# Mean-square pooling on one core: joined square roots, and one sum over groups of four for six of the twenty loads

## The chip, the core and the metric

The kernel runs on one core of a Trainium2 chip. Time is device time in microseconds (us) of one execution; of several executions the median is given. The profiled execution is a further one, and its trace covers a span that is somewhat shorter than its time.

## The reference

The input x has the shape (32, 256, 4096) in float32, p is 2.0 and the kernel size is 4. Each output is a power mean over four neighbours:

```python
for i in range(out_length):
    start = i * kernel_size
    end = start + kernel_size
    window = np.abs(x[:, :, start:end]) ** p
    result[:, :, i] = (np.mean(window, axis=-1)) ** (1.0 / p)
```

So out = sqrt((a*a + b*b + c*c + d*d) / 4): 134.22 MB are read from HBM and 33.55 MB are written, with four squares, three adds and one root for each output.

## The kernel before

**Tiles.** The flat input is cut into 20 loads: 19 of 128 partitions x 13184 values (6592 KB) and a last one of 11648. Three buffers of that size, xt0 to xt2 (`X_SLOTS = 3`), take them in turn, so load i+3 goes into the buffer of load i and can be issued only when load i has been summed. Output blocks 0 to 3 hold four loads each; their results stand side by side in one tile ot (4 x 3296 values a partition, `place`, line 69). One store of 6592 KB sends a block out. Loads 16, 17 and 18 form a fifth block and load 19 a sixth; their results go into the buffer of load 17, which no later load needs.

**Steps of a load.** ScalarE squares it in place (`square`, line 88). VectorE adds in two instructions: `pairs` (line 94) adds values 0 and 1 of each four to values 2 and 3, 13184 to 6592 in place; `fours` (line 98) adds the two that are left, 6592 to 3296. ScalarE takes the root with the scale 1/4 (`root`, line 101) into ot. Since ot is still being stored when the first load of the next block is ready, the sums of loads 4, 8, 12 and 16 go to a PSUM tile st (`summed`, line 103), and only the root moves them to ot, which then has to wait for the store. The sums of loads 5, 9 and 13 are the first to be written into ot by VectorE, and wait for the same store.

**Order.** The order is written by hand (`tc.manual_schedule()`); each engine works through its own list. In the loop over loads 0 to 16 (line 114), ScalarE does square(i) and then the root of load i-1; for i = 4, 8 and 12 the root of i-1 goes ahead of square(i), so that the store of the finished block can be issued. Stores 0 to 2 are issued by ScalarE's queue, right after the root that fills the block (line 108). SyncE's queue issues the loads, and after load 19 the stores 3, 4 and 5. An instruction in a queue waits behind those in front of it.

**Tail.** After the loop, load 17 is squared and summed, and loads 18 and 19 are squared by both engines: VectorE multiplies the first 4608 or 2000 values by themselves (line 134), ScalarE squares the others. Then come the last sums, roots and stores.

**Dependencies.** The waits follow from the tiles that instructions write and read. `tc.declare_no_dep` takes out one of them where others already ensure it; the kernel before uses it in `shared_pairs` alone.

Of the kernel before, what the change touches and what calls it, by code (L numbers as in the profile page):

```python
# [1 line left out]

# [4 lines left out]


@with_exitstack
def kernel(  # L10
    ctx: ExitStack,
    tc: tile.TileContext,
    x: bass.AP,
    p: float,
    kernel_size: int,
    out: bass.AP,
):

    nc = tc.nc

    assert float(p) == 2.0, "kernel specialized for p == 2"
    k = int(kernel_size)  # L30
    assert k == 4, "kernel specialized for kernel_size == 4"

    P = nc.NUM_PARTITIONS
    fp32 = mybir.dt.float32
    Act = mybir.ActivationFunctionType
    add = mybir.AluOpType.add
    xf = x.rearrange("b c l -> (b c l)")
    of = out.rearrange("b c l -> (b c l)")
    total = xf.shape[0] // P

    W = 13184
    R = W // k
    X_SLOTS = 3
    LAST = total - 19 * W
    widths = [W] * 19 + [LAST]
    n = len(widths)
    assert 0 < LAST <= W and LAST % 16 == 0


    blocks = [[0, 1, 2, 3], [4, 5, 6, 7], [8, 9, 10, 11], [12, 13, 14, 15], [18, 16, 17], [19]]  # L50
    block_of = {i: b for b, group in enumerate(blocks) for i in group}
    block_width = [sum(widths[i] for i in group) for group in blocks]

    x_pool = ctx.enter_context(tc.tile_pool(name="x_pool", bufs=1))
    o_pool = ctx.enter_context(tc.tile_pool(name="o_pool", bufs=1))
    s_pool = ctx.enter_context(tc.tile_pool(name="s_pool", bufs=1, space=bass.MemoryType.PSUM))
    x_tiles = [x_pool.tile([P, W], fp32, name=f"xt{j}") for j in range(X_SLOTS)]
    o_tile = o_pool.tile([P, 4 * R], fp32, name="ot")
    first = o_pool.tile([P, 1], fp32, name="first")
    s_tile = s_pool.tile([P, 4096], fp32, name="st")  # L60
    ctx.enter_context(tc.manual_schedule())

    def rows(flat, b, div):
        at = sum(block_width[:b]) * P // div
        return flat[at:at + block_width[b] * P // div].rearrange("(p w) -> p w", p=P)


    free = x_tiles[17 % X_SLOTS]
    place = {i: o_tile[:, i % 4 * R:(i % 4 + 1) * R] for i in range(16)}
    place[18] = free[:, R:2 * R]  # L70
    place[19] = free[:, 0:LAST // k]
    place[16] = free[:, 2 * R:3 * R]
    place[17] = free[:, 3 * R:4 * R]
    held = [o_tile[:, :]] * 4 + [free[:, R:4 * R], place[19]]

    xs, loads = {}, {}

    def load(i):
        b = block_of[i]
        at = sum(widths[j] for j in blocks[b][:blocks[b].index(i)])  # L80
        xs[i] = x_tiles[i % X_SLOTS][:, 0:widths[i]]
        loads[i] = nc.sync.dma_start(out=xs[i], in_=rows(xf, b, 1)[:, at:at + widths[i]])  # L82

    def store(b, queue):
        queue.dma_start(out=rows(of, b, k), in_=held[b])  # L85

    def square(v):
        return nc.scalar.activation(out=v, in_=v, func=Act.Square)  # L88

    def pairs(v):  # L90

        q = v.rearrange("p (n j) -> p n j", j=k)
        h = v[:, 0:v.shape[1] // 2].rearrange("p (n j) -> p n j", j=2)
        return nc.vector.tensor_tensor(out=h, in0=q[:, :, 0:2], in1=q[:, :, 2:4], op=add)  # L94

    def fours(o, v):
        h = v[:, 0:v.shape[1] // 2].rearrange("p (n j) -> p n j", j=2)
        return nc.vector.tensor_tensor(out=o, in0=h[:, :, 0], in1=h[:, :, 1], op=add)  # L98

    def root(o, s):  # L100
        nc.scalar.activation(out=o, in_=s, func=Act.Sqrt, scale=1.0 / k)  # L101

    summed = {i: s_tile[:, 0:R] if i in (4, 8, 12, 16) else place[i] for i in range(n)}

    def roots(i):
        root(place[i], summed[i])
        if i in (3, 7, 11):
            store(block_of[i], nc.scalar)

    for i in range(X_SLOTS):  # L110
        load(i)

    root(first[:, :], nc.const_aps.tensor(1.0, (P, 1), fp32))
    for i in range(17):
        ends = i in (4, 8, 12)
        if ends:
            roots(i - 1)
        square(xs[i])
        if i and not ends:
            roots(i - 1)  # L120
        pairs(xs[i])
        fours(summed[i], xs[i])
        if i + X_SLOTS < n:
            load(i + X_SLOTS)

    store(3, nc.sync)
    square(xs[17])
    pairs(xs[17])
    fours(summed[17], xs[17])
    later = {18: 4608, 19: 2000}  # L130

    def shared_square(i):
        v = xs[i][:, 0:later[i]]
        nc.vector.tensor_tensor(out=v, in0=v, in1=v, op=mybir.AluOpType.mult)  # L134
        square(xs[i][:, later[i]:widths[i]])

    def shared_pairs(i):
        tc.declare_no_dep(pairs(xs[i]).ins, loads[i].ins, reason="the two squares waited for it")

    shared_square(18)  # L140
    roots(16)
    roots(17)
    shared_pairs(18)
    fours(summed[18], xs[18])
    shared_square(19)
    roots(18)
    store(4, nc.sync)
    shared_pairs(19)
    fours(summed[19], xs[19])
    roots(19)  # L150
    store(5, nc.sync)


# [1 line left out]
_INS = ['x', 'p', 'kernel_size']  # L155
_OUTS = [((32, 256, 1024), 'float32')]

_NUMBERS = {'p': 2.0, 'kernel_size': 4}


# [26 lines left out]
```

## Time and profile before

| what | value |
|---|---|
| three executions | 394.27, 394.32, 394.55 us; median 394.32 us |
| profiled execution | 394.39 us |
| its span in the trace | 392.4 us |
| moved by DMA | 134.22 MB read and 33.55 MB written |
| ScalarE: 20 squares, 20 roots | 216.7 us and 58.6 us |
| VectorE: 20 `pairs`, 20 `fours`, 2 multiplications | 139.7, 71.5 and 7.2 us |

In profile lines ACT is ScalarE, DVE is VectorE, SP is SyncE; SPq and ACTq are their queues, which only wait and issue. L94 is line 94 of the kernel. A group of instructions reads: line, engine, operation, output <- input with partitions x elements and type, the count, then the busy time, the mean time of one in nanoseconds and the engine's idle time just before them with what ended it. A line of the timeline reads: start, length, engine, line, operation, names, and in brackets the idle time before it and what ended that. "Landing" of a DMA is the moment at which its semaphore tells that all of it has arrived.

### The profile page before, as it was taken

The page shows a single profiled execution, that of the slowest core. Times are in us where ns is not written, and L with a number is a line of the kernel's source. Part 1 is how long each engine was busy: PE and PEld are TensorE (multiplying, and loading weights), DVE is VectorE, ACT ScalarE, POOL GpSimd, SP SyncE. Part 2 cuts the span into 40 slices and gives each one's busy share as a digit, 9 for nine tenths or more (in the row PEclk, how much of TensorE's full clock was granted, in tenths as well). Part 3 has the DMA queues.
Part 4 walks back from the last instruction along what each step waited for, and adds up shares of the span by engine and source line. Part 5 has one row for each costly group of instructions (what it writes and reads, how often), then busy time and mean ns, then how long its engine had stood idle before and what let it go on. Part 6 is the DMA issues. An engine that isn't in the chain of part 4 may idle for free.

```text
span 392.4 us, 183 instructions
## 1 busy us (share of the span) xinstructions
DVE 218.2 (56%) x42; ACT 275.0 (70%) x42; POOL 0.2 (0%) x4
## 2 busy tenths in 40 slices
DVE  0009477490593265905942759069417586499980
ACT  1095988919950999199519891995298988969910
POOL 0000000000000000000000000000000000000000
DMA  8999999999999999999999999999999999999997
GB/s 344 430 430 430 430 446 441 446 446 371 430 430 430 430 430 430 446 430 441 446 441 435 441 441 430 430 435 430 430 430 430 430 430 430 430 452 414 430 425 329
DMA packets 3744, 167.77 MB, mean 428 GB/s; under 512 B 416, under 2 KB 416, under 8 KB 416
## 3 DMA queue, kind: packets, MB, share of 16 engines
q1 hardware_dynamic: 3312, 147.52, 87.4%
q10 hardware_dynamic: 432, 20.25, 11.9%
HBM read 134.22 MB, written 33.55 MB: 428 GB/s over the span
## 4 chain that ended last, share of the span: by engine, by line
DMA 42%; ACT 32%; DVE 23%; issue 0%; ACTq 0%; DVEq 0%; SPq 0%
DMA xt<-in_x_dram 33%; ACT xt L88 28%; DVE xt L94 14%; DMA out_dram<-ot 9%; DVE ot L98 5%; ACT ot L101 3%; DVE xt L98 3%; DVE xt L134 2%; ACT xt L101 1%; ACTq L85 0%; DVEq L94 0%; SPq L82 0%; ACTq L101 0%
## 5 line engine op out<-in xcount | busy, mean ns | idle before, releaser
L88 ACT ACTIVATE xt<-xt 128x13184 f32<-128x13184 f32 (+2 forms) x20 | 216.7, 10847 | 37.0 <-DMA xt<-in_x_dram 35.7
L94 DVE TENSOR_TENSOR xt<-xt 128x6592 f32<-128x6592 f32 (+1 forms) x20 | 139.7, 6986 | 144.8 <-ACT xt L88 144.6
L98 DVE TENSOR_TENSOR ot<-xt 128x3296 f32<-128x3296 f32 x13 | 46.7, 3592 | 17.4 <-DMA out_dram<-ot 17.1
L101 ACT ACTIVATE ot<-ot 128x3296 f32<-128x3296 f32 x13 | 38.2, 2938 | 23.6 <-DVE ot L98 23.6
L101 ACT ACTIVATE ot<-st 128x3296 f32<-128x3296 f32 x3 | 8.8, 2917 | 38.2 <-DMA out_dram<-ot 38.2
L101 ACT ACTIVATE xt<-xt 128x3296 f32<-128x3296 f32 (+1 forms) x3 | 8.5, 2840 | 8.8 <-DVE xt L98 8.8
L98 DVE TENSOR_TENSOR st<-xt 128x3296 f32<-128x3296 f32 x4 | 14.4, 3600 | 0.1
L98 DVE TENSOR_TENSOR xt<-xt 128x3296 f32<-128x3296 f32 (+1 forms) x3 | 10.4, 3458 | 0.1
L134 DVE TENSOR_TENSOR xt<-xt 128x4608 f32<-128x4608 f32 (+1 forms) x2 | 7.2, 3592 | 0.0
L101 ACT ACTIVATE xt<-st 128x3296 f32<-128x3296 f32 x1 | 2.9, 2897 | 0.0
L101 ACT ACT_TABLE_LOAD x1 | 1.3, 1283 | 0.7 <-PEq L168 0.7
L101 ACT ACTIVATE first<-const-float32-1.0 128x1 f32<-128x1 f32 x1 | 0.2, 202 | 0.0
L168 POOL MEMSET const-uint8-127<- 128x1 uint8 x1 | 0.1, 102 | 0.0
L168 POOL MEMSET const-bfloat16-1.0<- 128x1 bf16 x1 | 0.1, 101 | 0.0
L168 POOL MEMSET const-float32-0.0<- 128x1 f32 x1 | 0.1, 98 | 0.2 <-issue 0.2
L168 POOL MEMSET const-float32-1.0<- 128x1 f32 x1 | 0.1, 98 | 0.0
## 6 DMA issues: line engine op xcount, KB each, us to landing
xt<-in_x_dram SPq DMA_DIRECT2D x19, 6592.0 KB, 29.8
out_dram<-ot ACTq DMA_DIRECT2D x3, 6592.0 KB, 35.0
out_dram<-ot SPq DMA_DIRECT2D x1, 6592.0 KB, 38.1
xt<-in_x_dram SPq DMA_DIRECT2D x1, 5824.0 KB, 23.0
out_dram<-xt SPq DMA_DIRECT2D x1, 4944.0 KB, 16.1
out_dram<-xt SPq DMA_DIRECT2D x1, 1456.0 KB, 8.1
```

What stands on the lines that cost most here:

```text
L88: return nc.scalar.activation(out=v, in_=v, func=Act.Square)
L94: return nc.vector.tensor_tensor(out=h, in0=q[:, :, 0:2], in1=q[:, :, 2:4], op=add)
L98: return nc.vector.tensor_tensor(out=o, in0=h[:, :, 0], in1=h[:, :, 1], op=add)
L101: nc.scalar.activation(out=o, in_=s, func=Act.Sqrt, scale=1.0 / k)
L134: nc.vector.tensor_tensor(out=v, in0=v, in1=v, op=mybir.AluOpType.mult)
L168: nc = _bacc.Bacc("TRN2", target_bir_lowering=False, num_devices=1)
```

## The change

Three things differ; the loads, the tiles and the tail are the same.

1. **Roots are joined and moved.** Roots of neighbouring places in ot whose sums lie in ot are taken in one instruction over two or three places: loads 0, 1 and 2 behind square 3; 5 and 6 behind square 7; 9 and 10 behind square 11; 13 and 14 behind square 15. The single roots of loads 4 and 8 (from st) come right after the joined ones, that of 12 behind square 14, and those of 3, 7, 11 stay ahead of squares 4, 8 and 12, each followed by its store; root 15 comes behind square 16. In the kernel before, roots 4, 8 and 12 stood ahead of squares 6, 10 and 14.
2. **One sum over groups of four.** For loads 4, 7, 8, 11, 12 and 15, `pairs` and `fours` are replaced by one `tensor_reduce` that adds along the innermost axis of the view (3296 groups of 4): it reads 13184 values and writes 3296. For 4, 8 and 12 it writes to st in PSUM, for 7, 11 and 15 to ot. It doesn't write to the load's own buffer.
3. **Dependencies that others imply are taken out:** of squares 3, 7 and 11 on the sums that last used their buffer, and of the joined roots of blocks 1 and 2 on the store of the block before.

```diff
     def root(o, s):
-        nc.scalar.activation(out=o, in_=s, func=Act.Sqrt, scale=1.0 / k)
+        return nc.scalar.activation(out=o, in_=s, func=Act.Sqrt, scale=1.0 / k)
...
-    def roots(i):
-        root(place[i], summed[i])
-        if i in (3, 7, 11):
-            store(block_of[i], nc.scalar)
+    def roots(*group):
+        if len(group) == 1:
+            root(place[group[0]], summed[group[0]])
+        else:
+            v = o_tile[:, group[0] % 4 * R:(group[-1] % 4 + 1) * R]
+            r = root(v, v)
+            if group[0] in (5, 9):
+                implied(r, stores[block_of[group[0]] - 1])
+        if group[-1] in (3, 7, 11):
+            store(block_of[group[-1]], nc.scalar)
+
+    def implied(later, earlier):
+        tc.declare_no_dep(later.ins, earlier.ins, reason="implied by the other waits")
...
+    ahead = {4: (3,), 8: (7,), 12: (11,)}
+    behind = {3: [(0, 1, 2)], 7: [(5, 6), (4,)], 11: [(9, 10), (8,)], 14: [(12,)], 15: [(13, 14)], 16: [(15,)]}
...
     for i in range(17):
-        ends = i in (4, 8, 12)
-        if ends:
-            roots(i - 1)
-        square(xs[i])
-        if i and not ends:
-            roots(i - 1)
-        pairs(xs[i])
-        fours(summed[i], xs[i])
+        if i in ahead:
+            roots(*ahead[i])
+        s = square(xs[i])
+        if i in (3, 7, 11):
+            for earlier in sums[i - X_SLOTS]:
+                implied(s, earlier)
+        for group in behind.get(i, []):
+            roots(*group)
+        if i in (4, 7, 8, 11, 12, 15):
+            q = xs[i].rearrange("p (n j) -> p n j", j=k)
+            sums[i] = nc.vector.tensor_reduce(out=summed[i], in_=q, op=add, axis=mybir.AxisListType.X),
+        else:
+            sums[i] = pairs(xs[i]), fours(summed[i], xs[i])
         if i + X_SLOTS < n:
             load(i + X_SLOTS)
```

## The prediction

> **What bounds the kernel now.** I read the share of busy time first, and it misleads: no engine is near full, and the chain of waits spreads the end over transfers, ScalarE and VectorE.
>
> ```profile
> DVE 218.2 (56%) x42; ACT 275.0 (70%) x42; POOL 0.2 (0%) x4
> ...
> DMA packets 3744, 167.77 MB, mean 428 GB/s; under 512 B 416, under 2 KB 416, under 8 KB 416
> ...
> DMA 42%; ACT 32%; DVE 23%; issue 0%; ACTq 0%; DVEq 0%; SPq 0%
> ```
>
> The chain passes through a square and two sums whenever a load was issued just after them, but it does not say whether that load then had to wait behind another. So I cut the span into stretches and asked for the DMA share (columns: stretch, length, busy time of DVE, ACT and POOL, clock, DMA share, GB/s):
>
> ```profile
> 4.00:88.00 84.00, 42.47 (x8) 53.50 (x8) 0.00 (x0) 1.00 1.00 432
> 88.00:98.00 10.00, 0.00 (x0) 9.54 (x2) 0.00 (x0) 1.00 1.08 422
> 98.00:172.00 74.00, 42.48 (x8) 51.37 (x9) 0.00 (x0) 1.00 1.00 433
> 172.00:250.00 78.00, 42.48 (x8) 56.25 (x9) 0.00 (x0) 1.00 1.00 433
> 250.00:330.00 80.00, 45.36 (x9) 64.89 (x9) 0.00 (x0) 1.00 1.00 432
> ```
>
> A share of 1.00 in every long stretch: the 16 DMA engines never rest from 4 to 330 us. The kernel is bound by the rate of its transfers. The timeline gives that rate: squares 1, 2 and 3 wait for their loads and start at 34.70, 50.28 and 65.86, so a load of 6592 KB (6.75 MB) takes 15.58 us, 433 GB/s. All 167.77 MB take 387.2 us at that rate. The first load, issued at 0.73, lands at 19.11, so 18.38 - 15.58 = 2.8 us are start and landing; I use 2.8 as the lead by which a load must be issued before the one in front of it lands. 0.73 + 2.8 + 387.2 = 390.7, and the last store lands at 383.39 + 8.1 = 391.5. Only 0.8 us are lost anywhere. Where: square 3 starts at 65.86 and square 7 at 144.62, five transfers (loads 4 to 7, store 0) in 78.8 us instead of 77.9; the next five, to square 11 at 222.45, take 77.8. The loss is at the first store (422 GB/s from 88 to 98) and does not come back.
>
> The tail is full too: store 3 lands at 338.26 + 38.1 = 376.4, store 4 needs 4944/6592 of 15.58 = 11.7 and lands at 372.00 + 16.1 = 388.1, store 5 needs 3.4 and lands at 391.5. Each starts where the one in front ends.
>
> So the question for each edit is only: is some load or store issued so late that the queue runs dry?
>
> **The change, part by part.** The rows that are replaced and those from which the new ones are priced (count | busy, mean ns | idle before, releaser):
>
> ```profile
> L88 ACT ACTIVATE xt<-xt 128x13184 f32<-128x13184 f32 x18 | 201.1, 11186 | 31.9 <-DMA xt<-in_x_dram 30.6 <-ACT ot L101 1.3
> L94 DVE TENSOR_TENSOR xt<-xt 128x6592 f32<-128x6592 f32 x19 | 133.5, 7026 | 144.7 <-ACT xt L88 144.6
> L98 DVE TENSOR_TENSOR ot<-xt 128x3296 f32<-128x3296 f32 x13 | 46.7, 3592 | 17.4 <-DMA out_dram<-ot 17.1
> L101 ACT ACTIVATE ot<-ot 128x3296 f32<-128x3296 f32 x13 | 38.2, 2938 | 23.6 <-DVE ot L98 23.6
> L101 ACT ACTIVATE ot<-st 128x3296 f32<-128x3296 f32 x3 | 8.8, 2917 | 38.2 <-DMA out_dram<-ot 38.2
> ```
>
> **One sum for two.** Six times 7.03 + 3.59 = 10.65 us (with the gap) go; six reductions over 13184 values come, an operation that the trace does not show. Call its time D. From the rows: 7026 - 3592 ns for 6592 - 3296 outputs is 1.042 ns an output, plus 0.16 fixed. If the reduction goes by outputs, it is a line 98 row, 3.6; if it takes two inputs a step, as the two-input sums do, 7.0; one input a step, 13184 x 1.042 + 0.16 = 13.9; two steps an input, 27.6. I take 13.9, since a reduction has one input stream and the nearest rows move one element of each stream a step; 3.6 and 27.6 stay as ends. VectorE then has 6 x 3.25 = 19.5 us more work, and each slot comes free that much later. If it were all on the path, that would be +19.5.
>
> What hides it is the load or two already queued. In after, with landings moved only by the rule of 15.58 us:
>
> - Reduction 4 starts at 102.40; load 7 is issued at 102.40 + D = 116.3 (113.12 before). Load 6 lands 15.58 before load 7's 144.60, at 129.0; less 2.8 the limit is 126.2.
> - Reduction 7 starts at 155.84; load 10 at 169.7. Load 9 lands at 144.60 + 31.16 = 175.8; limit 173.0, that is D up to 17.1.
> - Root 7 (2.95), store 1 (0.42) and square 8 (11.2) then follow, so reduction 8 starts at 170.4 + D and load 11 is issued at 170.4 + 2D = 198.2 (191.84 before). Load 10 lands, with store 1 between, four transfers after 144.60, at 206.9; limit 204.1, D up to 16.8.
> - Reductions 11 and 12 likewise from 233.67: limits 17.1, and 248.2 + 2D against 222.43 + 62.3 - 2.8 = 281.9, D up to 16.8.
> - Reduction 15 starts at 311.54; load 18 at 325.4 (322.25 before). Load 17 lands at 331.47; limit 328.7, D up to 17.1.
>
> ```profile
> 311.41 2.93 ACT L101 ACTIVATE ot<-ot 128x3296 f32<-128x3296 f32 x1
> 311.54 7.03 DVE L94 TENSOR_TENSOR xt<-xt 128x6592 f32<-128x6592 f32 x1 [4.45 <-ACT xt L88]
> 315.90 11.19 ACT L88 ACTIVATE xt<-xt 128x13184 f32<-128x13184 f32 x1 [1.56 <-DMA xt<-in_x_dram]
> 318.60 3.59 DVE L98 TENSOR_TENSOR ot<-xt 128x3296 f32<-128x3296 f32 x1
> ```
>
> At 13.9 all margins are near 3 us or more, and at 3.6 or 7.0 they are larger. Cost and gain: 0.
>
> A page of the Trainium skill speaks against this edit: "VectorE: DVE Perf Modes", "The perf-mode tier table (the rule you actually need)" and "Rules for kernel authors" allow tensor_reduce one element a cycle only and advise against it on a hot path. At its 0.96 GHz that is an estimated 13.7 us, near my 13.9, which no row yet shows. By the page the six would cost 18 to 19 us; by the row of DMA shares this path is not hot, and they cost nothing.
>
> **Later stores.** Root 7 waits for the reduction, so stores 1 and 2 are issued 3.2 us later (169.50 to 172.8, 247.34 to 250.6). The sums 9 and 13 (line 98) wait for those stores to land, 35 us later, and loads 12 and 16 follow: 208.2 to 211.5, against a limit of 222.43 - 2.8 = 219.6. Hidden; the queue holds load 11 meanwhile.
>
> **Joined and moved roots.** Five ScalarE instructions go. The fixed part of one is 2.94 - 3296 x 0.83 = 0.2 us (0.83 ns from the squares of 13184 and 8576, 11.19 and 7.35), so 1.0 us of ScalarE. Roots 4, 8 and 12 no longer hold the next square until a store lands (the 38.2 us above). What is late next is the load: square 6 moves from 129.67 to the landing at 129.0, no further. The joined roots (0, 1, 2), (5, 6) and (9, 10) stand behind squares 3, 7 and 11, while VectorE still sums those loads: covered. The tight place is (13, 14), 2.94 + 2.74 = 5.7 us between squares 15 and 16: 311.5 + 5.7 = 317.2, so square 16 starts 1.3 late, ends at 328.4, root 15 ends at 331.4, just as load 17 lands (331.47). Sum 16, load 19 and, behind it on SP's queue, store 3 go out 1.3 us later (339.2 instead of 337.85); load 18 lands at 347.0. Hidden. If this cover failed, square 17 and the rest would shift; store 5 has 388.1 - 383.39 - 2.8 = 1.9 us of room before it shows.
>
> **Sum:** 392.4 + 0 span. The profiled execution took 394.39, 2.0 around the span, and stands 0.07 above the median of 394.32. **394.4.**
>
> **Rivals.**
> *Slower: the reduction is the pace.* One mechanism, at reductions 7/8, 11/12 and 15, deciding from D = 16.8: beyond it each pair costs 2 us per us (the second starts late by the first's delay and adds its own) and reduction 15 one, 5 in all. D = 18 gives +6, 400; D = 27.6 gives +54, 448. For it: every value is read singly in groups of four, and no row shows this operation. Against: line 98 reads with a step and still keeps 1.04 ns. 7 in 100, mostly its lower part.
> *Faster: the loss at the first store vanishes.* The transfers gain the 0.8 to 0.9 us: 393.5. For it: only there does the queue lose. Against: up to store 0 at 90.75 the new order issues everything at the same times (reduction 4 starts at 102.4). 3 in 100.
> *The operation is quick (3.6 or 7.0).* The change then does for VectorE what it says, slots come free up to 7 us earlier, and the queue is as full as before: 394.4 too. It belongs to the forecast.
>
> **How the numbers follow.** No change has 90 in 100, slower 7, faster 3; a measurement of this kernel tells about 0.2% (0.8 us) from none. The range goes from 393.5, the transfers without any loss, to 395.2, where the joined root's 1.3 us comes through in part. Other cases above it hold under 10 in 100.
>
> **What would show it.** DMA share 1.00 from 4 to 330; squares 7, 11, 15 and 17 starting at 144.6, 222.4, 300.3 and 331.5 again; a reduction row of about 13.9 us; the waits of roots for stores gone, those of squares for loads longer. Wrong if a stretch falls below 430 GB/s, or if square 11 starts late (reductions 7 and 8) or square 17 (the joined root).

## The result and the profile after

The changed kernel takes 407.23 us (median of 6 executions, 406.32 to 408.20), the kernel before 394.29 us (394.09 to 394.55): a ratio of 1.0329, 95% interval 1.0317 to 1.0340. The change costs 13 us; the prediction said 394.4, with a range up to 395.2. The profiled execution, one of the six, took 407.69 us, with a span of 405.9, 13.5 more than before. All executions reported here had a granted clock of 1.0.

The top of the page looks much as expected: VectorE is busier by 19.3 us, ScalarE does five instructions less.

```profile
DVE 237.5 (59%) x36; ACT 274.4 (68%) x37; POOL 0.2 (0%) x4
...
DMA packets 3744, 167.77 MB, mean 413 GB/s; under 512 B 416, under 2 KB 416, under 8 KB 416
...
DMA 42%; DVE 31%; ACT 24%; issue 0%; ACTq 0%; DVEq 0%; SPq 0%
```

The chain now gives VectorE 31% instead of 23%, and one could stop there and blame the reductions. The mean rate on the second line is the better lead: the same bytes at 413 GB/s instead of 428. The new operations cost what they were priced at (count | busy, mean ns | idle before):

```profile
L141 DVE TENSOR_REDUCE st<-xt 128x3296 f32<-128x13184 f32 x3 | 41.7, 13895 | 43.9 <-ACT xt L88 43.9
L141 DVE TENSOR_REDUCE ot<-xt 128x3296 f32<-128x13184 f32 x3 | 41.7, 13887 | 14.8 <-ACT xt L88 14.8
L101 ACT ACTIVATE ot<-ot 128x6592 f32<-128x6592 f32 x3 | 17.0, 5679 | 0.0
```

The stretches that the prediction read (stretch, length, busy DVE, ACT, POOL, clock, DMA share, GB/s) show where the time went:

```profile
4.00:88.00 84.00, 42.47 (x8) 53.31 (x6) 0.00 (x0) 1.00 1.00 432
...
98.00:172.00 74.00, 48.92 (x6) 48.58 (x7) 0.00 (x0) 1.00 1.00 433
172.00:250.00 78.00, 43.98 (x6) 53.64 (x7) 0.00 (x0) 1.00 1.00 406
250.00:330.00 80.00, 46.93 (x7) 57.40 (x8) 0.00 (x0) 1.00 1.00 424
```

The share is still 1.00 in each: the queue did **not** run dry from 172 to 330. But at the same share only 406 GB/s are moved from 172 to 250, where it was 433, and 424 behind that, where it was 432. The DMA engines are busy with packets that take longer. The timeline of the changed kernel dates it:

```profile
169.65 2.95 ACT L101 ACTIVATE ot<-ot 128x3296 f32<-128x3296 f32 x1 [5.56 <-DVE ot L141]
172.63 0.34 ACTq L85 DMA_DIRECT2D out_dram<-ot  x1
173.01 22.27 ACT L88 ACTIVATE xt<-xt 128x13184 f32<-128x13184 f32 x2 [0.42 <-ACT ot L101]
...
214.21 11.19 ACT L88 ACTIVATE xt<-xt 128x13184 f32<-128x13184 f32 x1 [18.93 <-DMA xt<-in_x_dram]
...
229.83 11.19 ACT L88 ACTIVATE xt<-xt 128x13184 f32<-128x13184 f32 x1 [4.43 <-DMA xt<-in_x_dram]
...
311.81 11.19 ACT L88 ACTIVATE xt<-xt 128x13184 f32<-128x13184 f32 x1 [1.56 <-DMA xt<-in_x_dram]
...
374.28 8.24 ACT L88 ACTIVATE xt<-xt 128x9648 f32<-128x9648 f32 x1 [2.72 <-DMA xt<-in_x_dram]
```

The rows of the kernel before for store 1 and squares 11, 15 and 19:

```profile
169.50 0.34 ACTq L85 DMA_DIRECT2D out_dram<-ot  x1
...
222.45 11.19 ACT L88 ACTIVATE xt<-xt 128x13184 f32<-128x13184 f32 x1 [1.05 <-DMA xt<-in_x_dram]
...
300.31 11.19 ACT L88 ACTIVATE xt<-xt 128x13184 f32<-128x13184 f32 x1 [1.07 <-DMA xt<-in_x_dram]
...
360.85 8.24 ACT L88 ACTIVATE xt<-xt 128x9648 f32<-128x9648 f32 x1 [0.79 <-DMA xt<-in_x_dram]
```

Up to store 1, issued at 172.63 (predicted 172.8), all is as predicted. Then load 10, awaited by square 10, lands at 214.2 instead of 206.9, and square 11 starts at 229.83 instead of 222.45: 7.4 us lost while store 1 and load 10 run side by side. Square 15 starts at 311.81 (before 300.31), so 4.1 more go at store 2; square 19 at 374.28 (360.85), 1.9 more when store 3 starts. That is 13.4 of the 13.5 us.

The packets of the trace show how. I strung them together, each to the one that starts where another ends, which gives 16 rows, one for each DMA engine (the trace does not name the engine, so the stringing is inferred). L is a packet of a load (52736 bytes, one row of one partition), S one of a store, | the 4-byte packet that ends a transfer; a number is the packet's time in us where it is over 1.97, all others take 1.95. A square waits for the semaphore of a load, so its start in the timeline shows when all rows of that load are done. Around store 1:

```
before, 11 of 16 rows    L L L L S | S L S L S L S L S L S L S L | L |
after, one of 15 rows    L L L L | L S2.1 L S2.5 L S2.7 L S2.6 L S2.6 L S2.7 L S2.6 L S2.5 | |
after, the exception     L L L L | L L S L2.5 S L S L S L S L3.2 S L S | S L |
```

Before, the store comes in ahead of the end of load 9, so a row of load 10 stands beside later rows of the store, and every packet takes 1.95 us (the other five rows begin L L L L S L S | S, likewise). After, the store comes in when each engine has done just one packet of load 10. From then on row k of the load is followed by row k of the store, **in step**, and mostly one of the two takes 2.1 to 3.8 us: in the row shown always the store's, in others the load's in part. Fifteen rows do this; the sixteenth drew one more load packet first and is mostly at 1.95.

### The profile page after: what moved, and what is told of

Same layout as the page of the kernel before. It is cut to its first block, busy times and chain, and to the rows that moved or that the text cites. A ratio compares the mean times of both kernels' runs of the same rounds, so it can differ in the third digit from the quotient of the medians.

```text
span 405.9 us, 172 instructions
## 1 busy us (share of the span) xinstructions
DVE 237.5 (59%) x36; ACT 274.4 (68%) x37; POOL 0.2 (0%) x4
## 4 chain that ended last, share of the span: by engine, by line
DMA 42%; DVE 31%; ACT 24%; issue 0%; ACTq 0%; DVEq 0%; SPq 0%
DMA xt<-in_x_dram 42%; ACT xt L88 22%; DVE xt L94 10%; DVE st L141 7%; DVE ot L141 7%; DVE ot L98 3%; DVE xt L98 3%; DVE xt L155 2%; ACT ot L101 1%; ACT xt L101 1%; ACTq L85 0%; DVEq L94 0%; SPq L82 0%
## 5 line engine op out<-in xcount | busy, mean ns | idle before, releaser
L94 DVE TENSOR_TENSOR xt<-xt 128x6592 f32<-128x6592 f32 (+1 forms) x14 | 97.5, 6967 | 76.3 <-ACT xt L88 76.1
L141 DVE TENSOR_REDUCE st<-xt 128x3296 f32<-128x13184 f32 x3 | 41.7, 13895 | 43.9 <-ACT xt L88 43.9
L141 DVE TENSOR_REDUCE ot<-xt 128x3296 f32<-128x13184 f32 x3 | 41.7, 13887 | 14.8 <-ACT xt L88 14.8
L98 DVE TENSOR_TENSOR ot<-xt 128x3296 f32<-128x3296 f32 x10 | 35.9, 3592 | 19.6 <-DMA out_dram<-ot 19.3
L101 ACT ACTIVATE ot<-ot 128x3296 f32<-128x3296 f32 (+2 forms) x8 | 37.2, 4656 | 13.5 <-DVE ot L141 11.1
L98 DVE TENSOR_TENSOR st<-xt 128x3296 f32<-128x3296 f32 x1 | 3.6, 3600 | 0.0
```

The costliest lines, as they stand in the source:

```text
L101: return nc.scalar.activation(out=o, in_=s, func=Act.Sqrt, scale=1.0 / k)
L141: sums[i] = nc.vector.tensor_reduce(out=summed[i], in_=q, op=add, axis=mybir.AxisListType.X),
```

## The experiments

Three theories: P, a store that starts in step with a load slows the packets of both; L, loads issued later run the queue dry somewhere; R, the reduction or the joined roots disturb the transfers themselves.

### 1. Only the stores later

```diff
+    def pause(i, times, width):
+        for _ in range(times):
+            nc.scalar.activation(out=s_tile[:, R:R + width], in_=place[i][:, 0:width], func=Act.Square)
+
     def roots(i):
+        if i in (7, 11):
+            pause(i, 4, 700)
         root(place[i], summed[i])
```

> The kernel before, with four short ScalarE operations (about 3.2 us together, outputs into an unused part of st) between the sum and the root of loads 7 and 11, so that only stores 1 and 2 (and the squares behind them) come as late as in the changed kernel: about 172.7 instead of 169.5 us. Theory P (a store that starts in step with a load, row for row on each DMA engine, makes the packets of both slow): 400 to 408, with packets of store 1 over 2.0 us and square 11 about 7 us late. Theory L (loads issued late by the long reductions run the queue dry): no load is issued much later than before, so 394.3. Theory R (the reduction or the joined roots disturb transfers themselves): 394.3.

Measured: 406.40 us (401.19 to 407.27), ratio 1.0265, interval 1.0194 to 1.0335. Nothing of the change is in this kernel but the time of stores 1 and 2 and of the squares behind them, and it loses nearly as much, 1.9 to 3.4%. Square 11 starts at 231.50, 9 us late where about 7 were expected. Store 1 of this kernel, then the stretch from 176 to 212 us in the kernel before and in this one:

```profile
172.60 0.34 ACTq L85 DMA_DIRECT2D out_dram<-ot  x1
```

```profile
176.00:212.00 36.00, 21.25 (x4) 23.59 (x4) 0.00 (x0) 1.00 1.02 441
```

```profile
176.00:212.00 36.00, 17.65 (x3) 19.25 (x2) 0.00 (x0) 1.00 1.01 378
```

Shares of 1.02 and 1.01, but 441 against 378 GB/s. P holds; L and R gave 394.3. That the squares come late cannot be the reason: in experiment 3 they come later still.

### 2. Only the loads later

```diff
+    stall = {4: 2950, 7: 2950, 8: 5900, 11: 2950, 12: 5900, 15: 2950}
...
         fours(summed[i], xs[i])
+        if i in stall:
+            v = xs[i][:, 0:stall[i]]
+            nc.vector.tensor_tensor(out=v, in0=v, in1=v, op=add)
```

> The kernel before, with one more VectorE addition on the dead buffer behind the sums of loads 4, 7, 8, 11, 12 and 15 (3.2 us, for 8 and 12 6.3 us), so that loads 7, 10, 11, 14, 15 and 18 are issued as late as in the changed kernel, while stores 0 to 2 stay where they were. Theory P: 394.3, within 0.8. Theory L: most of the 13 us, 400 to 408. Theory R: 394.3.

Measured: 394.33 us, ratio 1.0003 (0.9993 to 1.0012). Loads 10 and 11 went out at 169.65 and 198.00 (the two issues of the second row below), as in the changed kernel, store 1 at 169.33:

```profile
169.33 0.34 ACTq L85 DMA_DIRECT2D out_dram<-ot  x1
169.65 28.68 SPq L82 DMA_DIRECT2D xt<-in_x_dram  x2
```

The same stretch:

```profile
176.00:212.00 36.00, 27.46 (x5) 23.41 (x4) 0.00 (x0) 1.00 1.02 444
```

Theory L falls: as long as the stores are in time, the prediction's margins for the loads were right.

### 3. The changed kernel, its stores later still

`pause` is that of experiment 1.

```diff
+        if group[-1] in (7, 11):
+            pause(group[-1], 2, 790)
         if len(group) == 1:
             root(place[group[0]], summed[group[0]])
```

> The changed kernel, with two short ScalarE operations (1.7 us together) ahead of roots 7 and 11, so that stores 1 and 2 come 1.7 us later still, when each DMA engine has begun the second row of load 10: row k of the store then stands beside row k+1 or later of the load. Theory P: most of the loss goes, 394 to 397. Theory L: no better, 407 to 411. Theory R: 407 or a little more.

Measured: 394.40 us (394.06 to 396.06), ratio 1.0014 (1.0001 to 1.0027). Store 1 goes out at 174.23, 1.6 us after that of the changed kernel, and the loss of 13 us is gone. All 16 rows now read `L | L L S L S L ...`, at 1.95. Store 1 here, then the same stretch in the changed kernel and here:

```profile
174.23 0.34 ACTq L85 DMA_DIRECT2D out_dram<-ot  x1
```

```profile
176.00:212.00 36.00, 20.82 (x2) 19.28 (x2) 0.00 (x0) 1.00 1.01 376
```

```profile
176.00:212.00 36.00, 24.12 (x3) 28.16 (x3) 0.00 (x0) 1.00 1.02 442
```

All six reductions and all joined roots are in this kernel, so R falls too.

### 4. All transfers in one queue

```diff
-            store(block_of[group[-1]], nc.scalar)
+            store(block_of[group[-1]], nc.sync)
```

> The changed kernel, with stores 0 to 2 issued by SyncE's queue, in the order of the program, so that loads and stores run one behind the other and never packet by packet in turn. Theory P: 393.4 to 395, the loss at store 0 included if that has the same cause. Theory L: 407, for the loads are issued as late as in the changed kernel. Theory R: 407.

Measured: 395.22 us (394.42 to 395.71), ratio 1.0022 (1.0012 to 1.0031). Without a second queue there are no turns to take, and 12 us of the 13 are gone. It is 0.2 us over what P gave, and the loss at store 0 did not go: the packet ahead of it takes 2.1 to 3.2 us here too.

### 5 to 8. The change in parts

Experiments 5, 7 and 8 are the changed kernel with another condition on the sums in the loop: no reduction (5), reductions 4, 8, 12 and 15 (7), 7 and 11 (8). Experiment 6 is the kernel before, with its old roots, and all six reductions.

```diff
-        if i in (4, 7, 8, 11, 12, 15):
+        if i in ():
```

(This is experiment 5; it is `(4, 8, 12, 15)` in 7 and `(7, 11)` in 8.)

> The changed kernel with two sums for every load, so that only the joined and moved roots are left of the change. Stores 1 and 2 are issued at 169.5 and 247.3 us as in the kernel before. Theory P (store in step with a load): 394.3, within 0.8. Theory R (the joined roots disturb): 397 or more.

> The kernel before with one sum instead of two for loads 4, 7, 8, 11, 12 and 15, roots as before. Store 1 is issued at about 172.7 us, in step with load 10. Theory P: 400 to 408. If the loss needs the joined roots: 394.3.

> The changed kernel with one sum for loads 4, 8, 12 and 15 only: those that do not stand ahead of a store issued by ScalarE. Stores 1 and 2 come at 169.5 and 247.3 us. Theory P: 394.3, within 0.8. Theory R (the reduction disturbs transfers): about two thirds of the 13 us, 400 or more.

> The changed kernel with one sum for loads 7 and 11 only, those whose root is followed by a store. Stores 1 and 2 come at 172.7 and about 3 us late. Theory P: 400 to 408. Theory R: about a third of the 13 us, 397 to 399.

| kernel | store 1 issued | us | ratio, interval |
|---|---|---|---|
| 5, joined roots only | 169.25 | 394.14 | 0.9990, 0.9972 to 1.0007 |
| 6, reductions, old roots | 172.56 | 405.52 | 1.0285, 1.0258 to 1.0312 |
| 7, reductions 4, 8, 12, 15 | 169.38 | 394.12 | 0.9994, 0.9984 to 1.0003 |
| 8, reductions 7 and 11 | 172.66 | 406.37 | 1.0312, 1.0284 to 1.0339 |

All four as P said. Four of six reductions cost nothing; the two ahead of a store cost everything, through 3.3 us on that store. Reductions 7 and 11 are 3.2 us slower than the two sums, and what costs time in that is the moment alone.

### 9. Other HBM rows

```diff
-        stores[b] = queue.dma_start(out=rows(of, b, k), in_=held[b])
+        stores[b] = queue.dma_start(out=rows(of, {1: 2, 2: 1}.get(b, b), k), in_=held[b])
```

> The changed kernel with the places of blocks 1 and 2 in the output exchanged: store 1 goes to the HBM rows of block 2 and store 2 to those of block 1, 6.75 MB away; output blocks 1 and 2 are exchanged by this. Order, times and partitions stay. Theory P with the cause on the SBUF side (both packets use the same partition): 405 to 409 as before the exchange. Theory P with the cause in the HBM addresses of the two rows: another time, 394 to 403.

Measured: 406.78 us, ratio 1.0321 (1.0300 to 1.0342). The stretch from 176 to 212:

```profile
176.00:212.00 36.00, 20.82 (x2) 19.37 (x2) 0.00 (x0) 1.00 1.00 374
```

Moving the rows in HBM by 6.75 MB changes nothing. If loads and stores are spread over the DMA engines alike, row k of a load and row k of a store use the same partition of SBUF, so a conflict there would fit. That it is one was not shown: the trace does not name partitions, no kernel here paired rows in step on different ones, and one shift of the HBM address does not exclude every cause on that side. The order of the two matters as well: in experiment 11 two rows begin `| S L S L`, with row k of the store just ahead of row k of the load, and every packet of theirs takes 1.95.

### 10. A tiny store at the start

```diff
     root(first[:, :], nc.const_aps.tensor(1.0, (P, 1), fp32))
+    nc.scalar.dma_start(out=rows(of, 5, k)[:, 0:1], in_=first[:, :])
```

> The kernel before, with one more tiny store (128 x 1 values of the tile first, into the place that the last store fills later) issued by ScalarE's queue at about 2 us. If the packets of 2.2 to 3.4 us ahead of store 0 are a one-time cost of the first transfer from SBUF to HBM, it is paid while nothing else runs: 393.4 to 393.6. If they come from how store 0 meets load 5: 394.3.

Measured: 394.58 us, ratio 1.0007 (0.9998 to 1.0015). No gain: the slow packets ahead of store 0 are not a cost of the first transfer of its direction, and together with experiment 4 not one of the second queue. They stay unexplained.

### 11 and 12. The moment, dosed

The kernel before again, with the pause of experiment 1 at two other lengths: `pause(i, 2, 630)` and `pause(i, 6, 760)`.

> The kernel before, with stores 1 and 2 about 1.4 us later (two short ScalarE operations between sum and root of loads 7 and 11): store 1 at about 170.9 us. Theory P (slow only in step, when row k of the store stands behind row k of the load): the first store packet still comes ahead of load 10, so 394.3, within 1. A store that is the slower the later it comes: 398 to 402.

> The kernel before, with stores 1 and 2 about 5 us later (six such operations): store 1 at about 174.5 us. Theory P: every engine has begun two rows of load 10 when the first store packet comes, out of step, so 394.3, within 1.5. A store that is the slower the later it comes: 410 or more.

Experiment 11: 394.19, 403.81, 404.29 and 405.93 us; three of the four missed what was expected. The profiled execution is that of 403.81. Store 1 at 170.91 stands there on the edge of the window, and the packets say so: 11 rows begin `L S | S L` and two `L | S L`, all at 1.95; three begin `| L S2.1 L S2.2 L2.5` or nearly so. That in the execution of 394.19 no row was in step is likely, but it has no trace. The next two lines are the same stretch, and root 8, which waits for store 1:

```profile
176.00:212.00 36.00, 18.75 (x4) 18.67 (x3) 0.00 (x0) 1.00 1.02 431
```

```profile
210.90 2.92 ACT L101 ACTIVATE ot<-st 128x3296 f32<-128x3296 f32 x1 [17.33 <-DMA out_dram<-ot]
```

At 431 GB/s, where it was 441, the mean is hardly down, yet root 8 starts at 210.90 instead of 204.56, so store 1 lands 6 us late. Load 10 lands at 210.65 by its semaphore, 206.86 in the kernel before: about 4 us late. Of the 16 signals that make up this landing, 13 came by 206.74 and three from 209.92 to 210.65. A transfer lands when its **slowest** engine is done, and three engines in step are enough.

Experiment 12: 397.52 us (396.83 to 399.22), ratio 1.0087 (1.0062 to 1.0112); expected were 392.8 to 395.8. Store 1 at 174.46 was out of step as P said (435 GB/s from 176 to 212, rows `| L L S L S`). The rest is another cost: with squares 5 us later twice, ScalarE had no waiting time left, squares 15 to 17 ran without waiting for a load (305.98, 319.90, 333.82; before, the last waited for its load at 331.49), and loads went out late. From 312 to 320 us, in the kernel before and then here:

```profile
312.00:320.00 8.00, 7.97 (x2) 6.44 (x2) 0.00 (x0) 1.00 0.98 422
```

```profile
312.00:320.00 8.00, 4.73 (x2) 8.00 (x3) 0.00 (x0) 1.00 0.98 402
```

So a queue that is served too late does cost, as the prediction's rule had it, but here only beyond what the change did: square 18 starts 1.3 us late (348.40). Another 1.6 us are lost up to square 19 (363.83 instead of 360.85), and the packets show where: the last packet of load 19, just ahead of store 3, takes 2.4 to 3.3 us on every engine instead of the 1.72 of the others of this load, 3.33 on the engine that ends last. In the kernel before all packets there take 1.72. It looks like the slow packets ahead of store 0, and why it comes here is as open.

Store 1 at 169.5 costs nothing, at 170.9 mostly 10 us, at 172.6 11 to 13, at 174.2 nothing. By these points the window is between 1.7 and 4.7 us wide; a packet takes 1.95.

## Why the prediction was wrong

**Right:** what bounds the kernel. The 16 DMA engines are never idle for long, and the bytes over the rate give the time; only the rate was not the constant that I took it for.

**Right:** the price of the reduction, 13.9 from the rows, 13.89 measured. The page "VectorE: DVE Perf Modes" of the Trainium skill, section "The perf-mode tier table (the rule you actually need)", gave one element a cycle, an estimated 13.7; the runs agree (13.89). Its advice against the operation on a hot path (section "Rules for kernel authors") could be set aside for four of the six, which cost nothing in experiment 7; the other two delay a store, and there their 3.2 us did matter.

**Right:** the roots (5.7 predicted, 5.68 measured), load 11's issue (198.2, measured 198.16), store 1's issue (172.8, measured 172.63), and that all loads stay hidden while the stores are in time (experiment 2).

**Wrong, and the whole of it:** the step "Later stores ... Hidden". It put the effect of stores 1 and 2 being issued 3.2 us later at nothing. Experiment 1, with that and the squares behind it alone, measured about 12 us, and the changed kernel with both stores moved out of step (experiment 3) loses 0.1 us of 13. I asked when the store is issued and who waits for its landing, and moved every landing "only by the rule of 15.58 us". That rule came from loads that run alone and from stores that in this kernel had always met a load out of step. I knew that a store of ScalarE's queue shares the DMA engines with the loads of SyncE's queue, but not how. The Trainium skill has the missing half, "DMA: Bandwidth & Descriptors", section "Queues, rings and completion order": each engine takes turns between the queues, a packet at a time. The rows L S L S agree. These runs show besides that the turns may fall in step, and what this costs. Why packets in step are slow stays open (experiment 9). From the rows before, 1.95 us in every packet of stores 0 to 2 with the store's row ahead, it could not be derived; but a store moved by 3.2 us against a packet of 1.95 was a change to a pairing that no row of before had shown, and it deserved a term with both ends instead of "Hidden".

**Wrong for the same reason:** load 10 landing "four transfers after 144.60, at 206.9"; it took 214.2. And the rule that a load is early enough if issued 2.8 us before the one in front lands: after store 1 the engines are several us apart. In the changed kernel, while load 17's last packets come:

```profile
334.00:342.00 8.00, 5.22 (x2) 8.00 (x2) 0.00 (x0) 1.00 0.80 310
```

Most engines had finished load 17 and waited for load 18, with one still at work. It cost nothing more, since the slowest engine set each landing from square 15 on: its packets, followed back through the trace, exceed 1.95 us by 4.2 in all at store 2, where it alone is in step, and one packet of load 19, shortly ahead of store 3, takes 3.76 instead of the 1.72 of its neighbours, 2.0 more. Those are, within 0.1 us, the 4.1 and 1.9 us of the account above.

**The rivals:** "the reduction is the pace" needed 16.8 us and was rightly not it; its 7 in 100 stood for the right sign by the wrong mechanism. None of the rivals let a transfer become slower. Of the tests named for being wrong, a stretch below 430 GB/s is the one that showed it (406). A late square 11 came true too (229.83), but the reason put beside it, reductions 7 and 8, was not the cause: experiment 3 has both and takes 394.40 us.

**No better version was found:** with the joined roots alone (394.14), or reductions out of a store's way (394.12), the kernel stands at the rate of its transfers, as the kernel before does.

## What to carry to other kernels

In a kernel bound by transfers, read the rate beside the DMA share: a share of 1.00 says that the engines are occupied, not that they move what they can. A store from a second queue is a partner of the load that runs beside it; an edit that moves its issue by a packet's time is a change in its own right, and a short pause in front of it tests that cheaply. A transfer lands with its slowest engine, so a disturbance of three engines in sixteen (experiment 11) delays everything that waits for it.

## What the runs showed of the hardware

- Load and store of the same shape in two queues, row k of the store right behind row k of the load on an engine: mostly one of the two packets of 52736 bytes takes 2.1 to 3.8 us instead of 1.95, and the two transfers together move 376 GB/s instead of 441. With the store one row further back (experiment 3), or with its row ahead of the load's (the kernel before; two rows in experiment 11), packets keep 1.95.
- The packet ahead of the first large store takes 2.1 to 3.4 us on each engine, in one queue or in two, and a tiny store before it does not change that. Ahead of store 3, behind load 19 in the same queue, the same was seen in the changed kernel (2.4 to 3.8 us instead of 1.72) and in experiment 12, not in the kernel before. There it came on all engines at one moment (the slow packets of the changed kernel start from 366.0 to 366.8 us), also on the engine that was two packets behind. The cause is open.
- A transfer lands with its slowest engine: of the 16 signals of load 10 in experiment 11, 13 had come by 206.74 us, the last came at 210.65.
- A tensor_reduce over 128 x 3296 groups of 4 float32 takes 13.89 us, to SBUF or to PSUM, against 10.65 for two tensor_tensor additions.
